# Eleven modulations of a two-layer diffusion block as scaled row sums on VectorE, ScalarE and GpSimd

## Chip, cores and metric

The kernel runs on one core of a Trainium2 chip. The metric is the device time of one execution in microseconds (us), as the median of three runs. Engines are named as the profile names them: PE is TensorE's matmuls, PEld its weight loads, DVE is VectorE, ACT is ScalarE, POOL is GpSimd, SP is SyncE, whose queue here only issues transfers. A name like L252 is line 252 of the kernel before; the changed kernel has other line numbers, and where its lines are named it is said.

## The reference, cut to what matters

Two layers run over 256 latent and 256 context tokens of width 1024. Every layer is a half-step gated feed-forward (FFN), a token mixer, and a second FFN. Shift, scale and gate of each come from nine modulations per layer, each a matrix-vector product with a 1024x1024 slice of `w_mod`, once for the latent tokens' vector `c` and once for the context tokens' vector `c_ctx`:

```
mx = (silu(c) @ w_mod[l] + b_mod[l]).reshape(BATCH, 9, 1, 1024)
mc = (silu(c_ctx) @ w_mod[l] + b_mod[l]).reshape(9, 1024)
hx = hx + 0.5 * mx[:, 2] * swiglu(modulate(hx, norm_g[l, 0], mx[:, 0], mx[:, 1]), ffn_w_gu[l, 0], ffn_w_down[l, 0])
...
def swiglu(x, w_gu, w_down):
    gate, up = jnp.split(x @ w_gu, 2, axis=-1)
    return (jax.nn.silu(gate) * up) @ w_down
```

In the second layer the context tokens are only read by the mixer, so its last modulations (index 5 and up) are needed for the latent tokens alone.

## The kernel before, in words

All 512 tokens lie in one tile, features on the partitions. A float32 matmul is done as three matmuls of type fp32r (`mm3`, L291 to L293): weights and activations are split into a rounded high part and the low remainder, and the three are high by high, high by low, and low by high. The first operand is the weight: L291 and L292 read the high half of the weight, `spl[:, 0]`, and only L293 its low half, `spl[:, 1]`.

The weights come through a single list of units, written by `plan`, in the order in which they are consumed:

- a `gu` unit is 128 gate columns and 128 up columns of `ffn_w_gu` (1 MB in two transfers); an FFN has 22 of them, and each feeds 48 matmuls into two accumulators, first the gate's 24, then the up's 24;
- a `down` unit is 256 columns of `ffn_w_down`; an FFN has three chunks of four, after gu 7, gu 15 and gu 21;
- a `mod` unit is 256 columns of one modulation (1 MB), four to a modulation; they are strewn as fillers between the `gu` and `down` units, in the FFNs' parts of the list one filler behind each.

`take` (consumption of a unit) does three things: it issues loads up to three units on from the one taken (`load_to`), makes sure that the unit's own weight is split (`split`, L251 the high part on ACT, L252 the low part on DVE, each in two halves of 128x1024), and calls `ahead`, which splits the next weight unit early. `ahead` looks at two units from the cursor on and no further:

```
j = self.cur
n = min(j + 2, len(self.units))
while j < n and not self.units[j][3]:
    j += 1
if j < n:
    self.split(j)
```

Units that need no split (`mod`) are stepped over. So with one filler between two weight units, taking weight unit i splits weight unit i+1.

In `ffn`, after the 48 matmuls of a gu, come the gate's silu on ACT (`sl`, L667, needs the gate's accumulator only), the product with the up accumulator on DVE (`hv`, L669, needs the last of the 48 matmuls), its rounded copy on ACT (`hid`, L671), its remainder on POOL (L672), and then `fillers`, which consumes all fillers up to the next weight unit. After a `down` unit come four residual updates on DVE (`resid`, L729, two for each of the two accumulators), then the fillers. Work of the S5 preparation and deferred pieces are put between the matmuls by `step`, five times per gu and about four times per down.

A mod unit (`mod_unit`, L467) is eight matmuls of 128x32 by 128x256 in four column strips, into one bank for the four units of a modulation; after the fourth, a copy to SBUF (`mev`, L471), two transposes (L486) and a few short DVE instructions (`mod_finish`) bring the sums into place.

Of the kernel before, what the change touches and what calls it, by code (L numbers as in the profile page):

```python
# [33 lines left out]
PI_LO = 3.1415925  # L34

# [58 lines left out]
class Net:  # L94
    def __init__(self, nc, tc, I, out, es):
# [19 lines left out]
        self.mh = c.tile([128, 8], F32, name="mh")  # L115
        self.mod = [c.tile([128, 9, KT, 2], F32, name=f"mod{l}") for l in range(2)]
# [4 lines left out]
        self.units = []  # L121
        self.bg = []
# [14 lines left out]
    def plan(self):  # L137
# [140 lines left out]

    def fillers(self):
        while self.cur < len(self.units) and self.units[self.cur][0] == "mod":  # L280
            self.mod_unit(*self.units[self.cur][1])

    def fill(self, n):
        while n and self.cur < len(self.units) and self.units[self.cur][0] == "mod":
            self.mod_unit(*self.units[self.cur][1])
            n -= 1
# [18 lines left out]
    def step(self, n=1):  # L305

        for _ in range(n):
            f = self.q.pop(0) if self.q else None
# [5 lines left out]
    def flush(self):  # L314
        while self.q:
            f = self.q.pop(0)
            if f is not None:
                f()

# [5 lines left out]
    def prologue(self):  # L325
        nc, I = self.nc, self.I
        self.norm_open()
        with lines(self.tc, name="pro", bufs=1) as pp:
# [12 lines left out]
            nc.vector.memset(self.mh, -0.5)  # L341
            self.small_rows(0, sm[0])
# [138 lines left out]

    def mod_finish(self, l, m, us, e):
# [10 lines left out]
        if m in (1, 4, 7):  # L493
            g0 = 72 + 8 * (m // 3)
            g = self.smT[l][:, g0 + k0:g0 + k1].unsqueeze(2)
            nc.vector.scalar_tensor_tensor(self.A[l][:, m // 3, k0:k1], dst, 1.0, bc(g, [128, 2 * n, 2]), op0=OP.add, op1=OP.mult)
        if m in (2, 8):
            nc.vector.tensor_scalar(dst, dst, 0.5, None, op0=OP.mult)
# [146 lines left out]
    def ffn(self, l, f, halves, started, nxt=None):  # L645
# [5 lines left out]
        with lines(self.tc, name=f"ffn{l}{f}", bufs=1) as fp:  # L651
            j0 = 0
            for ci, nf in enumerate(CH):
# [26 lines left out]
                early = None  # L680
                for u in range(4):
# [43 lines left out]
                j0 += nf  # L725

# [855 lines left out]
```

## Time and profile before

| what | value |
|---|---|
| median of three runs (lowest to highest) | 1961.87 us (1960.69 to 1962.42) |
| the profiled execution, its own time | 1962.65 us |
| its span, first to last instruction | 1960.7 us |
| mean granted TensorE clock, share of full | 0.988 |
| PE busy | 1907.6 us, 97% |
| DVE, ACT, POOL busy | 907.3, 678.8, 574.3 us |
| chain that ended last: PE, DVE, POOL | 84%, 6%, 4% |

The profiled execution lies 0.8 us above the median, and 1.95 us of its time lie outside the span. The layers follow one another: prologue to about 65 us, then FFN, mixer, FFN for each layer. Busy shares are averages over the span; the chain of work that ended last says which engine the end waits for.

### The profile page before, as it was taken

To read this page: it belongs to the slowest core of one execution; us is meant where nothing else is said; L and a number is where in the kernel's file an instruction comes from. 1 tells how busy PE (TensorE), PEld (TensorE's weight loads), DVE (VectorE), ACT (ScalarE), POOL (GpSimd) and SP (SyncE) were. 2 spreads that over 40 slices of the span, in tenths; PEclk is the share of its full clock that TensorE was granted. 3 is DMA by queue.
4 is the path that set the end of the run, shared out by engine and by line. 5 is a ranking of instruction groups with operands and counts; after the bars stand their busy time and mean duration, and the time that the engine had idled before them with its cause. 6 is when DMAs were issued, how large, how long until landed. Compare 5 with 4: busy or idle time off the path is not lost.

```text
span 1960.7 us, 28001 instructions
## 1 busy us (share of the span) xinstructions
PE 1907.6 (97%) x11345; PEld 1557.8 (79%) x11345; DVE 907.3 (46%) x1596; ACT 678.8 (35%) x1128; POOL 574.3 (29%) x661
## 2 busy tenths in 40 slices
PE   7999999999999999999999999999999988999999
PEld 4777777788896587788888877777788878579999
DVE  6453233246457835232333554423433745655555
ACT  4421222224355634222212342122223435445343
POOL 2137461124535032100101314746212545231000
PEclk9999999999999999999999999999999999799999
DMA  9656566534431024533232455656523453036563
GB/s 309 178 166 200 174 205 212 165 97 141 132 105 51 2 86 130 173 117 96 88 105 76 139 158 167 201 160 217 178 75 113 141 166 100 22 126 215 175 194 108
DMA packets 364100, 277.75 MB, mean 142 GB/s; under 512 B 29854, under 2 KB 355812, under 8 KB 363972
## 3 DMA queue, kind: packets, MB, share of 16 engines
q1 hardware_dynamic: 361008, 268.44, 44.3%
q0 software_dynamic: 1888, 7.31, 1.0%
q8 instruction: 89, 1.46, 0.3%
q10 hardware_dynamic: 1076, 0.22, 0.1%
q14 instruction: 39, 0.32, 0.0%
HBM read 263.39 MB, written 12.55 MB: 141 GB/s over the span
## 4 chain that ended last, share of the span: by engine, by line
PE 84%; DVE 6%; POOL 4%; DMA 2%; ACT 1%; SPq 1%; issue 1%; POOLq 0%; ACTq 0%; DVEq 0%
PE acc L291 24%; PE acc L292 24%; PE acc L293 23%; PE b L467 3%; PE acc L1458 2%; PE t L1490 1%; DVE xm L562 1%; PE t L1510 1%; POOL ss L1134 1%; DVE xn L572 1%; PE acc L1463 1%; POOL sqs L523 1%; PE t L1100 1%; DMA bias<-in_na_rpb 1%; DVE xn L570 1%
## 5 line engine op out<-in xcount | busy, mean ns | idle before, releaser
L291 PE MATMUL acc<-xn,spl 128*128 128x512 f32 (+1 forms) x1664 | 598.0, 359 | 8.2 <-ACT mv L1340 5.9
L292 PE MATMUL acc<-xn,spl 128*128 128x512 f32 (+1 forms) x1664 | 590.7, 355 | 1.9 <-DVE xn L396 0.2
L293 PE MATMUL acc<-xn,spl 128*128 128x512 f32 (+1 forms) x1664 | 587.3, 353 | 0.1
L252 DVE TENSOR_TENSOR spl<-raw,spl 128x1024 fp32r<-128x1024 f32 (+2 forms) x312 | 390.2, 1287 | 276.0 <-ACT spl L251 273.8
L251 ACT ACTIVATE spl<-raw 128x1024 fp32r<-128x1024 f32 (+3 forms) x344 | 324.0, 990 | 303.9 <-PE acc L293 159.6
L291 PEld LDWEIGHTS acc<-xn,spl 128*128 128x128 f32 x1664 | 315.1, 189 | 71.7 <-issue 17.8
L292 PEld LDWEIGHTS acc<-xn,spl 128*128 128x128 f32 x1664 | 315.3, 189 | 46.7 <-DVE xn L570 4.3
L672 POOL TENSOR_TENSOR hid<-hv,hid 128x512 fp32r<-128x512 f32 (+1 forms) x88 | 101.8, 1156 | 852.2 <-ACT hid L671 852.2
L293 PEld LDWEIGHTS acc<-xn,spl 128*128 128x128 f32 x1664 | 315.3, 189 | 44.7 <-DVE spl L252 0.9
L291 PE MATMUL acc<-hid,spl 128*128 128x512 f32 (+1 forms) x740 | 265.2, 358 | 0.0
L292 PE MATMUL acc<-hid,spl 128*128 128x512 f32 (+1 forms) x740 | 262.0, 354 | 0.0
L293 PE MATMUL acc<-hid,spl 128*128 128x512 f32 (+1 forms) x740 | 261.7, 354 | 0.0
L669 DVE TENSOR_TENSOR hv<-sl,acc 128x512 f32<-128x512 f32 (+1 forms) x88 | 54.7, 621 | 365.1 <-PE acc L293 353.4
L671 ACT ACTIVATE hid<-hv 128x512 fp32r<-128x512 f32 (+1 forms) x88 | 50.9, 579 | 382.0 <-DVE hv L669 382.0
L729 DVE SCALAR_TENSOR_TENSOR h<-acc,mod,h 128x256 f32<-128x256 f32 x192 | 85.0, 479 | 210.8 <-PE acc L293 210.8
L291 PEld LDWEIGHTS acc<-hid,spl 128*128 128x128 f32 x740 | 139.8, 189 | 25.2 <-issue 6.4
L293 PEld LDWEIGHTS acc<-hid,spl 128*128 128x128 f32 x740 | 139.9, 189 | 19.7
L292 PEld LDWEIGHTS acc<-hid,spl 128*128 128x128 f32 x740 | 140.0, 189 | 18.5
L252 POOL TENSOR_TENSOR spl<-raw,spl 128x768 fp32r<-128x768 f32 (+3 forms) x32 | 65.3, 2041 | 211.4 <-ACT spl L251 199.5
L291 PE MATMUL acc<-spl,xn 128*128 128x384 f32 (+1 forms) x322 | 111.5, 346 | 0.0
L292 PE MATMUL acc<-spl,xn 128*128 128x384 f32 (+1 forms) x322 | 106.9, 332 | 0.4 <-POOL spl L252 0.3
L293 PE MATMUL acc<-spl,xn 128*128 128x384 f32 (+1 forms) x322 | 106.5, 331 | 0.0
(358 smaller groups left out, 1996.8 us busy)
## 6 DMA issues: line engine op xcount, KB each, us to landing
raw<-in_ffn_w_gu SPq DMA_DIRECT2D x176, 512.0 KB
raw<-in_w_mod SPq DMA_DIRECT2D x64, 1024.0 KB
raw<-in_ffn_w_down SPq DMA_DIRECT2D x32, 1024.0 KB
raw<-in_ffn_w_down SPq DMA_DIRECT2D x16, 768.0 KB
raw<-in_w_in SPq DMA_DIRECT2D x16, 768.0 KB
pmod<-in_w_mod SPq DMA_DIRECT2D x8, 1024.0 KB
raw<-in_w_out SPq DMA_DIRECT2D x8, 1024.0 KB
cld<-CL POOLq DMA_DIRECT2D x8, 576.0 KB, 4.8
```

The source lines that it names most:

```text
L251: nc.scalar.activation(s[:, 0, a:b], raw[:, a:b], AF.Copy)
L252: (nc.gpsimd if mix and b == n else nc.vector).tensor_tensor(s[:, 1, a:b], raw[:, a:b], s[:, 0, a:b].bitcast(F32), op=OP.subtract)
L291: mm(out, sl[0], sr[0], start=start, stop=False)
L292: mm(out, sl[0], sr[1], start=False, stop=False)
L293: mm(out, sl[1], sr[0], start=False, stop=stop)
L467: nc.tensor.matmul(p[32 * j:32 * j + 32, 0:256], self.cs[:, k, 6 - 2 * w:38 - 2 * w], raw[:, k, :], start=(a == 0 and w == 0), stop=(a == ...
L523: nc.gpsimd.tensor_tensor(self.sq_sum[:, c], self.sq_sum[:, c], s[:, c], op=OP.add)
L669: nc.vector.tensor_tensor(hv[:, c], sl[:, c], pu[:, c], op=OP.mult)
L671: nc.scalar.activation(hd[:, 0, c], hv[:, c], AF.Copy)
L672: nc.gpsimd.tensor_tensor(hd[:, 1, c], hv[:, c], hd[:, 0, c].bitcast(F32), op=OP.subtract)
L729: self.nc.vector.scalar_tensor_tensor(self.h[:, n, c], ps[:, c], self.mod[l][:, gate, n, s:s + 1], self.h[:, n, c], op0=OP.mult, op1=OP.add)
L1458: mm(s, q[:, 256 + 128 * t:384 + 128 * t], k, start=True, stop=h >= 6)
```

## The change

Eleven of the eighteen modulations (`ELEM`) leave the PE path. Each of their fillers, one mod unit of 256 columns and all eight row blocks before, becomes two `dvm` units of 512 columns and two row blocks (0.5 MB each), in the same place of the list. They have buffers of their own, `draw` (three, in the pool of the FFN), in place of the three `raw` buffers shared with the weights.

A dvm unit multiplies each of its two row blocks by the vector's value of that partition: for the latent tokens with one DVE instruction that also adds to a running sum `dacc1`, for the context tokens with an ACT copy with a scale (in place in `draw`) and an addition on POOL into `dacc0`. After four units (one half of a modulation) `total` puts four matmuls of 128x32 by 128x256 on PE, which add up the 128 partitions against a column of ones, and ACT copies the result; `finish` transposes it twice and adds the bias. `total` runs eight steps after the unit, `finish` three later. The two modulations (1,5) and (1,7) do the latent tokens alone. In the S5 preparation some scratch tiles now share a buffer, to make room.

```diff
+ELEM = ((0, 2), (0, 4), (0, 3), (0, 5), (0, 7), (0, 6), (1, 0), (1, 4), (1, 3), (1, 5), (1, 7))
...
         def mod_units(l, m, us=range(4)):
             for u in us:
+                if (l, m) in ELEM:
+                    for v in (2 * u, 2 * u + 1):
+                        n0, k0 = m * 1024 + v // 4 * 512, v % 4 * 2
+                        src = I["w_mod"][l].rearrange("(k p) n -> p k n", p=128)[:, k0:k0 + 2, n0:n0 + 512]
+                        U.append(("dvm", (l, m, v), [(slice(0, 1024), 2, src)], False))
+                    continue
...
+            if kind == "dvm" and self.fp is None:
+                return
             if i < 10 and kind == "mod":
                 raw = self.prop.tile([128, 2048], F32, name="pmod", tag="pmod", bufs=5)
+            elif kind == "dvm":
+                raw = self.fp.tile([128, 1024], F32, name="draw", tag="draw", bufs=3)
...
     def step(self, n=1):
         for _ in range(n):
+            if self.dv:
+                g = self.dv.pop(0)
+                if g:
+                    g()
...
+    def dvm_unit(self, l, m, v):
+        nc = self.nc
+        half, r = v // 4, v % 4
+        raw = self.take("dvm", (l, m, v)).rearrange("p (k n) -> p k n", k=2)
+        ss = (1,) if l and m > 4 else (0, 1)
+        if r == 0:
+            self.dacc = {s: self.fp.tile([128, 512], F32, name=f"dacc{s}", tag=f"dacc{s}", bufs=2) for s in ss}
+        acc = self.dacc
+        for i in range(2):
+            c0, c1 = (self.cs[:, 2 * r + i, 6 + s:7 + s] for s in range(2))
+            first = r == i == 0
+            if first:
+                nc.vector.tensor_scalar(acc[1], raw[:, i], c1, None, op0=OP.mult)
+            else:
+                nc.vector.scalar_tensor_tensor(acc[1], raw[:, i], c1, acc[1], op0=OP.mult, op1=OP.add)
+            if 0 in ss:
+                x = acc[0] if first else raw[:, i]
+                nc.scalar.activation(x, raw[:, i], AF.Copy, scale=c0)
+                if not first:
+                    nc.gpsimd.tensor_tensor(acc[0], acc[0], x, op=OP.add)
...
+        def total():
+            p = self.tp()
+            for j in range(2):
+                for s in range(2):
+                    z = 0 if s in ss else 1
+                    nc.tensor.matmul(p[64 * j + 32 * s:64 * j + 32 * s + 32, 0:256], self.sel[:, z:z + 32], acc[1 if z else s][:, 256 * j:256 * j + 256], start=True, stop=True)
+            st["e"] = self.modp.tile([128, 256], F32, name="mev", tag="mev")
+            nc.scalar.activation(st["e"], p[:, 0:256], AF.Copy)
...
+        self.dv_flush()
+        self.dv += [None] * 7 + [total, None, None, finish]
```

`take` and `ahead` are as before, and the instructions come out in another order. In the names of the rows below, `acc` is an accumulator of PE, `spl` a split weight, `hv` and `sl` the FFN's product and silu, `raw` a weight as loaded, `draw` a modulation's rows as loaded, `h` the residual stream.

DVE before, first FFN of layer 0, gu 8 to gu 10 (the accumulators named are those of the up halves):

```order
L669 TENSOR_TENSOR hv_1716<-sl_1714,acc_1646 128x512
L252 TENSOR_TENSOR spl_1734<-raw_1731,spl_1734 128x1024 x2
L669 TENSOR_TENSOR hv_1805<-sl_1803,acc_1740 128x512
L252 TENSOR_TENSOR spl_1825<-raw_1822,spl_1825 128x1024 x2
L491 TENSOR_REDUCE mod0_86<-t_1841 128x16
L492 TENSOR_TENSOR mod0_86<-mod0_86,smT0_90 128x16
```

DVE in the changed kernel, the same place:

```order
L758 TENSOR_TENSOR hv_1806<-sl_1804,acc_1744 128x512
L266 TENSOR_TENSOR spl_1814<-raw_1811,spl_1814 128x1024 x2
L530 TENSOR_SCALAR dacc1_1820<-draw_1728,cs_84 128x512
L532 SCALAR_TENSOR_TENSOR dacc1_1820<-draw_1728,cs_84,dacc1_1820 128x512
L532 SCALAR_TENSOR_TENSOR dacc1_1820<-draw_1741,cs_84,dacc1_1820 128x512 x2
L758 TENSOR_TENSOR hv_1920<-sl_1918,acc_1837 128x512
L266 TENSOR_TENSOR spl_1928<-raw_1925,spl_1928 128x1024 x2
```

Both show a product `hv`, then a split. Which gu the split is for stands in the rows of PE.

PE before, where gu 9 (acc_1740) ends and gu 10 (acc_1830) begins:

```order
L293 MATMUL acc_1740<-xn_83,spl_1640 128x512
L467 MATMUL b_1540<-raw_1721,cs_84 32x256 x8
L291 MATMUL acc_1830<-xn_83,spl_1734 128x512
L292 MATMUL acc_1830<-xn_83,spl_1734 128x512
L293 MATMUL acc_1830<-xn_83,spl_1734 128x512
```

PE in the changed kernel, where gu 8 (acc_1744) ends and gu 9 (acc_1836) begins:

```order
L313 MATMUL acc_1744<-xn_83,spl_1717 128x512
L314 MATMUL acc_1744<-xn_83,spl_1717 128x512
L312 MATMUL acc_1836<-xn_83,spl_1814 128x512
L313 MATMUL acc_1836<-xn_83,spl_1814 128x512
L314 MATMUL acc_1836<-xn_83,spl_1814 128x512
```

Before, spl_1734 stands on DVE behind the product of gu 8 and is read by gu 10, a whole gu later. In the changed kernel spl_1814 stands behind the product of gu 8 and is read by gu 9, the very next matmul.

ACT in the changed kernel, behind the same gu 8:

```order
L756 ACTIVATE sl_1804<-acc_1743 128x512
L760 ACTIVATE hid_1808<-hv_1806 128x512
L265 ACTIVATE spl_1814<-raw_1811 128x1024 x2
L535 ACTIVATE dacc0_1819<-draw_1728,cs_84 128x512
L535 ACTIVATE draw_1728<-draw_1728,cs_84 128x512
L535 ACTIVATE draw_1741<-draw_1741,cs_84 128x512 x2
```

The high part of the next weight now stands behind the copy `hid`, which reads `hv`.

DVE behind the down units of that chunk, changed kernel (acc_1535 and acc_1536 are down unit 2, and spl_1617 is read by down unit 3, acc_1639 and acc_1640):

```order
L822 SCALAR_TENSOR_TENSOR h_82<-acc_1535,mod0_87,h_82 128x256 x2
L822 SCALAR_TENSOR_TENSOR h_82<-acc_1536,mod0_87,h_82 128x256 x2
L266 TENSOR_TENSOR spl_1617<-raw_1615,spl_1617 128x1024 x2
L530 TENSOR_SCALAR dacc1_1623<-draw_1520,cs_84 128x512
L532 SCALAR_TENSOR_TENSOR dacc1_1623<-draw_1520,cs_84,dacc1_1623 128x512
L532 SCALAR_TENSOR_TENSOR dacc1_1623<-draw_1533,cs_84,dacc1_1623 128x512 x2
L822 SCALAR_TENSOR_TENSOR h_82<-acc_1639,mod0_87,h_82 128x256 x2
```

Before, the split behind the residual updates of down unit 2 was that of gu 8, a whole unit further on; now it is that of down unit 3.

## Rows read from the trace of the kernel before

**Rows 1.** The page's first part: busy time, share and instructions of each engine.
```profile
PE 1907.6 (97%) x11345; PEld 1557.8 (79%) x11345; DVE 907.3 (46%) x1596; ACT 678.8 (35%) x1128; POOL 574.3 (29%) x661
```
**Rows 2.** Timeline 206 to 208 us: start, duration, engine, line, names, [idle before <- releaser].
```profile
206.17 0.39 PE L293 MATMUL acc<-xn,spl 128*128 128x512 f32 x1
206.49 1.07 PE L467 MATMUL b<-raw,cs 128*32 128x256 f32 x16
...
206.67 0.69 DVE L669 TENSOR_TENSOR hv<-sl,acc 128x512 f32<-128x512 f32 x1 [8.16 <-PE acc L293]
207.39 0.64 ACT L671 ACTIVATE hid<-hv 128x512 fp32r<-128x512 f32 x1 [2.46 <-DVE hv L669]
...
207.49 0.50 PE L291 MATMUL acc<-xn,spl 128*128 128x512 f32 x1
...
207.83 0.40 PE L292 MATMUL acc<-xn,spl 128*128 128x512 f32 x1
```
**Rows 3.** Timeline of PE, 209 to 210.5 us, around two transposes of a modulation.
```profile
209.47 0.39 PE L293 MATMUL acc<-xn,spl 128*128 128x512 f32 x1
209.70 0.38 PE L486 MATMUL t<-k,mev 128*128 128x128 f32 x2
209.84 0.48 PE L291 MATMUL acc<-xn,spl 128*128 128x512 f32 x1
```
**Rows 4.** Timeline of DVE, 195 to 221 us: the splits around that product.
```profile
195.90 2.62 DVE L252 TENSOR_TENSOR spl<-raw,spl 128x1024 fp32r<-128x1024 f32 x2 [1.65 <-ACT spl L251]
...
216.06 3.21 DVE L252 TENSOR_TENSOR spl<-raw,spl 128x1024 fp32r<-128x1024 f32 x2 [8.70 <-ACT spl L251]
```
**Rows 5.** Groups by line and shape: names, count, busy us, mean ns, idle before.
```profile
L252 DVE TENSOR_TENSOR spl<-raw,spl 128x1024 fp32r<-128x1024 f32 x252 | 327.3, 1338 | 220.5 <-ACT spl L251 218.7 <-issue 1.8
L729 DVE SCALAR_TENSOR_TENSOR h<-acc,mod,h 128x256 f32<-128x256 f32 x192 | 85.0, 479 | 210.8 <-PE acc L293 210.8
...
L251 ACT ACTIVATE spl<-raw 128x1024 fp32r<-128x1024 f32 x260 | 259.9, 1047 | 281.5 <-PE acc L293 146.8 <-DMA raw<-in_ffn_w_gu 58.8 <-issue 43.9
L671 ACT ACTIVATE hid<-hv 128x512 fp32r<-128x512 f32 x66 | 41.7, 632 | 319.6 <-DVE hv L669 319.6
...
L523 POOL TENSOR_TENSOR sqs<-sqs,sq 128x512 f32<-128x512 f32 x20 | 28.6, 1430 | 81.9 <-ACT sq L522 73.6 <-issue 8.0
```
**Rows 6.** Windows, gap and stretch behind: length, busy us (instructions) by engine, PEclk, DMA, GB/s.
```profile
537.30:540.00 2.70, 0.03 (x2) 0.01 (x2) 2.21 (x2) 0.00 (x0) 2.23 (x2) 0.92 0.00 0
540.00:547.00 7.00, 6.93 (x24) 6.44 (x25) 1.77 (x2) 3.04 (x5) 1.87 (x1) 0.54 0.60 175
598.60:602.00 3.40, 0.00 (x0) 0.00 (x0) 1.84 (x4) 1.18 (x4) 2.81 (x3) 0.85 0.00 0
602.00:609.00 7.00, 6.99 (x26) 5.68 (x27) 4.83 (x13) 4.19 (x7) 6.04 (x6) 0.58 0.00 0
...
1596.00:1598.30 2.30, 0.01 (x1) 0.00 (x0) 2.30 (x4) 0.00 (x0) 1.11 (x2) 1.00 0.21 77
1598.30:1605.00 6.70, 4.96 (x27) 4.16 (x28) 3.13 (x7) 1.99 (x3) 5.36 (x7) 0.75 0.01 1
...
1761.20:1762.80 1.60, 0.08 (x8) 0.06 (x8) 1.02 (x3) 1.00 (x2) 1.09 (x2) 1.00 1.11 361
1762.80:1769.00 6.20, 6.12 (x56) 5.34 (x57) 6.04 (x14) 3.81 (x8) 1.69 (x2) 1.00 1.12 336
```
**Rows 7.** Timeline of PE behind the gap that ended at 602 us.
```profile
603.02 0.63 PE L293 MATMUL acc<-xn,spl 128*128 128x512 f32 x1
603.45 0.63 PE L291 MATMUL acc<-xn,spl 128*128 128x512 f32 x1
```
**Rows 8.** Windows: the first FFN of layer 0 as a whole, columns as in rows 6.
```profile
70.00:480.00 410.00, 407.68 (x2329) 321.43 (x2322) 164.93 (x311) 116.35 (x166) 152.51 (x183) 1.00 0.54 170
```
**Rows 9.** Timeline of SP's queue, 199 to 222 us: the issue of a gu weight.
```profile
219.30 1.07 SPq L228 DMA_DIRECT2D raw<-in_ffn_w_gu  x2
```
**Rows 10.** Timeline of ACT, 205 to 232 us: the split that waited for that weight.
```profile
225.17 2.01 ACT L251 ACTIVATE spl<-raw 128x1024 fp32r<-128x1024 f32 x2 [4.27 <-DMA raw<-in_ffn_w_gu]
```

More of the change, by code (lines that the diff above doesn't have):

```diff
@@ L121, in __init__ @@
         self.units = []
+        self.dv = []
+        self.fp = None
         self.bg = []
@@ L277, in ahead, with filler @@
             self.split(j)
+    def filler(self):
+        if self.cur == len(self.units) or self.units[self.cur][0] not in ("mod", "dvm"):
+            return False
+        kind, key = self.units[self.cur][:2]
+        (self.mod_unit if kind == "mod" else self.dvm_unit)(*key)
+        return True
     def fillers(self):
-        while self.cur < len(self.units) and self.units[self.cur][0] == "mod":
-            self.mod_unit(*self.units[self.cur][1])
+        while self.filler():
+            pass
     def fill(self, n):
-        while n and self.cur < len(self.units) and self.units[self.cur][0] == "mod":
-            self.mod_unit(*self.units[self.cur][1])
+        while n and self.filler():
             n -= 1
@@ L318, in flush, with dv_flush @@
                 f()
+    def dv_flush(self):
+        while self.dv:
+            g = self.dv.pop(0)
+            if g:
+                g()
     def drain(self):
@@ L480, in mod_unit, with finish @@
             self.q.append(lambda: self.mod_finish(l, m, us, e))
+    def dvm_unit(self, l, m, v):
[18 more added lines that the diff above has]
+                    nc.gpsimd.tensor_tensor(acc[0], acc[0], x, op=OP.add)
+        if r < 3:
+            return
+        st = {}
+        def total():
[6 more added lines that the diff above has]
+            nc.scalar.activation(st["e"], p[:, 0:256], AF.Copy)
+        def finish():
+            q = self.tp()
+            for i in range(2):
+                nc.tensor.transpose(q[:, 128 * i:128 * i + 128], st["e"][:, i * 128:i * 128 + 128], self.ident)
+            k0 = 4 * half
+            dst = self.mod[l][:, m, k0:k0 + 4]
+            t = q[:, 0:256].rearrange("p (a j s r) -> p a j s r", a=2, j=2, s=2)[:, :, :, :, 0]
+            b = self.smT[l][:, m * 8 + k0:m * 8 + k0 + 4].rearrange("p (j a) -> p a j", a=2).unsqueeze(3)
+            nc.vector.tensor_tensor(dst.rearrange("p (j a) s -> p a j s", a=2), t, bc(b, [128, 2, 2, 2]), op=OP.add)
+            self.mod_derived(l, m, k0, k0 + 4)
+        self.dv_flush()
+        self.dv += [None] * 7 + [total, None, None, finish]
@@ L482, in mod_finish, with mod_derived @@
+    def mod_derived(self, l, m, k0, k1):
+        nc = self.nc
+        dst = self.mod[l][:, m, k0:k1, :]
+        if m in (1, 4, 7):
+            g0 = 72 + 8 * (m // 3)
+            g = self.smT[l][:, g0 + k0:g0 + k1].unsqueeze(2)
+            nc.vector.scalar_tensor_tensor(self.A[l][:, m // 3, k0:k1], dst, 1.0, bc(g, [128, k1 - k0, 2]), op0=OP.add, op1=OP.mult)
+        if m in (2, 8):
+            nc.vector.tensor_scalar(dst, dst, 0.5, None, op0=OP.mult)
     def mod_finish(self, l, m, us, e):
@@ L680, in ffn @@
                 early = None
+                if lastc:
+                    self.dv_flush()
                 for u in range(4):
```

18 lines of the change are left out of this document (10 added, 8 removed).

## Prediction

> **What bounds the kernel now.** The page comes first: PE is busy 97% of the span, no other engine half of it [rows 1]. Next I read the stretch that the change touches, the first FFN of layer 0: of 410 us PE is busy 407.7, and DVE 165, ACT 116 and POOL 153 are spare capacity [rows 8]. On that page alone the change looks sure to pay: it takes work from the full engine and gives it to idle ones. Then I read one seam between two gu units at the scale of single instructions [rows 2]. The last matmul of a gu starts at 206.17. DVE's product needs it and starts at 206.67, after 8.16 us of idling; ACT's copy follows at 207.39. PE meanwhile does a mod unit and starts the next gu at 207.49, because that gu's weight was split long before, from 195.90 to 198.52 [rows 4]. So PE is never held up by the chain product, copy, split. It would be if the split came behind the product. That is what decides here.
>
> **What is removed.** A mod unit holds up PE as follows: from the last L293 at 206.17 to the next L291 at 207.49 are 1.32 us, and to the L292 behind it another 0.34 [rows 2]. Undisturbed, one matmul follows the other by 0.23 us (209.47 to 209.70) [rows 3]. So it costs 1.32 - 0.23 + 0.34 - 0.23 = 1.2 us. Eleven modulations have 44 of them: -53 us. Each was on PE's path, for PE is dense there [rows 8].
>
> **What is added on PE.** Each half modulation, 22 in all, adds up partitions with four matmuls of 128x32 by 128x256; a mod unit has eight of them in 1.07 us [rows 2], so 0.54 us, and with the 0.11 us by which the next matmul comes late, 0.65. 22 of them: +14 us. The pair of transposes costs 209.84 - 209.47 - 0.23 = 0.14 and some 0.1 behind it [rows 3]; there are 22 pairs and were 11: +2.6 us. PE alone gains 53 - 14 - 2.6 = **36 us**.
>
> **What is added elsewhere.** DVE gets 16 multiply-adds of 128x512 per modulation, 176. Nothing like them stands in the trace; the nearest are the product on 128x512 at 0.69 us [rows 2] and the residual update on 128x256 at 0.479, doubled 0.96 [rows 5]. I take 0.8: 141 us on an engine that is 46% busy. ACT gets 144 scaled copies at 0.632 [rows 5], 91 us; POOL 126 additions at 1.43 [rows 5], 180 us. In the first FFN, with six of the modulations, that is 77, 61 and 120 us beside 165, 116 and 153 in more than 410 us [rows 8]: each engine has room. Their cover is PE's work; none of it is on the path by volume. The order matters more.
>
> **The split comes late.** `ahead` looks at two units. With one filler behind a gu it reaches the next gu; with two dvm units it does not. So the next weight is split only when the first dvm unit is taken, which stands behind the gu's product on DVE and behind its copy on ACT. The orders above show it for gu and for down units.
>
> Behind a gu, with PE's last matmul starting at 206.17: product until 207.36, copy until 208.03 [rows 2], high half on ACT 1.05 us, until 209.1 [rows 5], low half on DVE 1.34 us, until 210.4 [rows 5]. L291 and L292 can start at 209.1; L293, which needs the low half, at 210.45. Undisturbed, that L293 would have started three steps of 0.23 behind 206.17, at 206.86. PE loses **3.5 us** (3.2 if splits and copies touch). The second half of the split is ready 1.3 us later, while PE has nine more matmuls, 2.1 us, before it needs it. Nothing else is queued on PE there.
>
> Behind a down unit ACT is free and does the high half in time. On DVE the last two residual updates start 0.5 us behind 206.17 and take 0.96, the low half 1.34 [rows 5]: 209.0 against 206.86, so **2.15 us**.
>
> From the plan's list: of the 44 pairs, 32 stand behind a gu (16 in the first FFN of layer 0, 4 in its second, 12 in the first of layer 1) and 12 behind a down unit. 32 x 3.5 + 12 x 2.15 = **138 us**. Both engines take their instructions in order: in the rows nothing passes the waiting product. The Trainium skill says so as a rule (TensorE: Matmul & The Clock Gate, "Architectural detail"): ScalarE and VectorE are strict FIFOs. By it the 138 us stand; if the split could pass the product, only the -36 would be left.
>
> **PE's clock.** Each of those waits leaves PE idle from 206.6 to 209.1, 2.5 us, then busy with two matmuls, then idle for 0.7 more. Such gaps exist in the trace [rows 6]. Behind 2.7, 3.4 and 2.3 us the granted clock of the next 7 us was 0.54, 0.58 and 0.75, and matmuls followed each other by 0.43 us in place of 0.23 [rows 7]: the lower of the two levels, 1.2 instead of 2.4 GHz. Behind a gap of 1.6 us it stayed at 1.00. The gap at 598.60 is the nearest: dense matmuls on both sides. Of the 7 us behind it 42% are lost, 2.9 us. My wait is between the two kinds, as two matmuls lie in it; its 3.2 us of idling are nearer the upper. I let the clock fall in two of three of the 32: 21 x 2.9 = **62 us**, and in none of the 12. The ends are 0 and 44 x 2.9 = 128. [...]
>
> **Transfers.** Bytes are the same. The weights have three buffers for themselves, but SP's queue is in order, and a weight stands behind a `draw` that waits until POOL has released the one three before. That release comes about 9.5 us behind the gu's end (split 5.6, two multiply-adds, two scaled copies partly beside them, two additions of 1.43); a weight landed 4.8 us after its issue had ended [rows 9, 10]. Together 15 to 16 us, against the 16.5 us until the next split wants it (11.1 us of matmuls, 3.5 of waiting, 1.9 to the split). Barely covered: 0 in the sum, up to 1 us in each of 32, +32, at the upper end, if POOL is late.
>
> **Sum.** The profiled execution took 1962.65 us, 0.04% above the median. 1962.65 - 36 + 138 + 62 = **2127 us**, +8.4%.
>
> **Rivals.**
> - *The waits without the clock.* Two matmuls inside each wait may be enough to hold it: 1962.65 - 36 + 138 = 2065. For it: the 1.6 us gap at full clock. Against: 2.3 us was enough at 1596. Chance 0.25.
> - *POOL and the transfers decide.* If draws come free late, weights do too and each wait grows: 2127 + 32, and with the clock lost behind nearly every wait up to 2205. For it: POOL's release chain above. Against: POOL has over 100 us spare in the first FFN [rows 8]. Chance 0.15.
> - *The waits do not appear, and PE's saving shows.* Place: the split's position behind the product. If DVE and ACT finish the split before PE has ended the gu, only -36 is left: 1927 us. It decides from an average of 36 / 44 = 0.8 us per pair; below that the kernel gets faster. For it: PE at 97% and idle engines. Against: the product needs the up half's last matmul, and DVE's idle time before it ends with just that, 8.16 us on PE's L293 [rows 2]. Chance 0.06.
> - *Nothing changes*, because waits and saving cancel within 0.2%, some 4 us (what a measurement of this kernel can tell from no change): 0.01.
>
> **Numbers.** The forecast has what is left, 0.53. Slower by over 0.2%: 0.53 + 0.25 + 0.15 = 0.93; same 0.01; faster 0.06. The range takes in the waits at their shorter value without the clock (32 x 3.2 + 12 x 2.15 = 128, so 2055) and the third case up to 2205. Outside lie the faster case and a little on either side.
>
> **What would show it.** In the changed profile PE should wait in its 32 places for ACT's and DVE's split of `spl` (about 2.5 and 0.7 us), and in 12 for DVE's alone; before it hardly ever waits for them. DVE's long idle before `hv` on PE stays, the one before the split goes. The strip of PE's clock, 9s before, should fall to 7 or 8 in the slices of the first FFNs of both layers (3 to 9 and 24 to 29) and stay in the others. Wrong would be the count of pairs, if PE waits elsewhere; the 3.5 us, if the wait per pair differs; the 62 us, if the clock stays at 1.00 there. If the end comes below 1960, the order read above did not bind.

## The result and the profile after

The changed kernel takes 2189.14 us in the median (2185.16 to 2195.32), the kernel before on the same chip 1961.61 us (1960.69 to 1962.42): a ratio of 1.1163, interval 1.1136 to 1.119. It is slower, by 228 us; 2127 had been forecast, in a range of 2055 to 2205. The profiled execution took 2195.32 us. The profile page of the changed kernel, parts 1 and 2, engines and clock:

```profile
span 2193.5 us, 27710 instructions
...
PE 1984.7 (90%) x10839; PEld 1600.1 (73%) x10839; DVE 1109.0 (51%) x1777; ACT 784.7 (36%) x1283; POOL 767.9 (35%) x789
...
PEclk9888888899999999989999998888899999899999
```

PE was busy for 1907.6 us [rows 1] and is for 1984.7, though 11 modulations less pass through it; that is the first sign of the clock. Its idle time went from 53 to 209 us (span less busy time). A slice of the strip is 55 us here. The 8s stand in slices 2 to 8, most of the first FFN of layer 0, in 18, its second, and in 25 to 29, the first of layer 1. The strip of before is 9 in all of these; both have one 7 or 8 in slice 35. Slice 18, with 4 of the 44 pairs, was not among those that the forecast named. The windows view of the first FFN's stretch, columns as in [rows 6]:

```profile
70.00:480.00 410.00, 325.52 (x1319) 242.87 (x1319) 206.82 (x321) 143.89 (x198) 236.29 (x234) 0.87 0.44 136
```

Against [rows 8], PE's busy time there is 325 in place of 408 us. 1319 matmuls in place of 2329 were done; some of the missing ones are the modulations' own, but of the three of `mm3` alone it is 1105 in place of 1659. What PE waits for stands in its list of waits of the changed kernel (engine, tile, line, what it waits for; us in total, times, longest):

```profile
PE acc L312 <- ACT spl L265: 116.7, 40, 5.5
PE acc L314 <- DVE spl L266: 31.2, 41, 1.6
PE t L1064 <- POOL CL L1057: 8.8, 2, 5.0
```

The two splits hold 148 us of the 156 us of new idle time. In the list of the kernel before, waits for a split come to about 1 us; the longest line is this:

```profile
PE t L292 <- DVE spl L252: 0.8, 1, 0.8
```

One seam between two gu units, in the timeline of the changed kernel, set against [rows 2]:

```profile
122.75 0.40 PE L314 MATMUL acc<-xn,spl 128*128 128x512 f32 x1
...
122.98 0.38 PE L554 MATMUL b<-k,mev 128*128 128x128 f32 x2
123.28 0.69 DVE L758 TENSOR_TENSOR hv<-sl,acc 128x512 f32<-128x512 f32 x1 [2.94 <-PE acc L314]
124.00 0.63 ACT L760 ACTIVATE hid<-hv 128x512 fp32r<-128x512 f32 x1 [4.92 <-DVE hv L758]
124.54 1.99 ACT L265 ACTIVATE spl<-raw 128x1024 fp32r<-128x1024 f32 x2
...
125.61 2.58 DVE L266 TENSOR_TENSOR spl<-raw,spl 128x1024 fp32r<-128x1024 f32 x2 [1.64 <-ACT spl L265]
...
125.63 0.50 PE L312 MATMUL acc<-xn,spl 128*128 128x512 f32 x1 [2.27 <-ACT spl L265]
...
127.12 0.80 PE L314 MATMUL acc<-xn,spl 128*128 128x512 f32 x1 [0.75 <-DVE spl L266]
127.71 0.63 PE L312 MATMUL acc<-xn,spl 128*128 128x512 f32 x1
128.14 0.63 PE L313 MATMUL acc<-xn,spl 128*128 128x512 f32 x1
```

Product, copy, high half, low half: the chain is read off line by line. From the last L314 of the old gu to the first L314 of the new one are 127.12 - 122.75 = 4.37 us. Less the 0.69 of three undisturbed steps and the 0.24 of the two transposes, 3.4 us are lost; the forecast had 3.5. Behind it matmuls follow each other by 0.43 us: half clock.

### The profile page after: what moved, and what is told of

It is laid out like the page before. It is cut to its first block, busy times and chain, and to the rows that moved or that the text cites. A ratio compares the mean times of both kernels' runs of the same rounds, so it can differ in the third digit from the quotient of the medians.

```text
span 2193.5 us, 27710 instructions
## 1 busy us (share of the span) xinstructions
PE 1984.7 (90%) x10839; PEld 1600.1 (73%) x10839; DVE 1109.0 (51%) x1777; ACT 784.7 (36%) x1283; POOL 767.9 (35%) x789
## 5 line engine op out<-in xcount | busy, mean ns | idle before, releaser
L312 PE MATMUL acc<-xn,spl 128*128 128x512 f32 (+1 forms) x1664 | 625.3, 376 | 96.3 <-ACT spl L265 87.9
L314 PE MATMUL acc<-xn,spl 128*128 128x512 f32 (+1 forms) x1664 | 617.2, 371 | 20.7 <-DVE spl L266 20.7
L313 PE MATMUL acc<-xn,spl 128*128 128x512 f32 (+1 forms) x1664 | 611.6, 368 | 1.9 <-DVE xn L429 0.2
L312 PEld LDWEIGHTS acc<-xn,spl 128*128 128x128 f32 x1664 | 329.0, 198 | 164.9 <-ACT spl L265 98.7
L314 PEld LDWEIGHTS acc<-xn,spl 128*128 128x128 f32 x1664 | 327.4, 197 | 89.0 <-DVE spl L266 40.0
L313 PEld LDWEIGHTS acc<-xn,spl 128*128 128x128 f32 x1664 | 329.1, 198 | 54.6 <-DVE xn L658 4.3
L312 PE MATMUL acc<-hid,spl 128*128 128x512 f32 (+1 forms) x740 | 273.3, 369 | 28.8 <-ACT spl L265 28.8
L314 PE MATMUL acc<-hid,spl 128*128 128x512 f32 (+1 forms) x740 | 270.0, 365 | 10.5 <-DVE spl L266 10.5
L313 PE MATMUL acc<-hid,spl 128*128 128x512 f32 (+1 forms) x740 | 268.8, 363 | 0.0
L537 POOL TENSOR_TENSOR dacc<-dacc,draw 128x512 f32<-128x512 f32 x126 | 187.2, 1485 | 158.7 <-ACT draw L535 106.8
L312 PEld LDWEIGHTS acc<-hid,spl 128*128 128x128 f32 x740 | 144.0, 195 | 55.4 <-ACT spl L265 32.5
L314 PEld LDWEIGHTS acc<-hid,spl 128*128 128x128 f32 x740 | 144.3, 195 | 37.4 <-DVE spl L266 16.5
L532 DVE SCALAR_TENSOR_TENSOR dacc<-draw,cs,dacc 128x512 f32<-128x512 f32 x154 | 164.0, 1065 | 4.7
L313 PEld LDWEIGHTS acc<-hid,spl 128*128 128x128 f32 x740 | 144.5, 195 | 20.0
L535 ACT ACTIVATE draw<-draw,cs 128x512 f32<-128x512 f32 x126 | 91.0, 724 | 131.4 <-DVE dacc L532 83.2
```

Source lines behind the costliest of these rows:

```text
L312: mm(out, sl[0], sr[0], start=start, stop=False)
L313: mm(out, sl[0], sr[1], start=False, stop=False)
L314: mm(out, sl[1], sr[0], start=False, stop=stop)
L532: nc.vector.scalar_tensor_tensor(acc[1], raw[:, i], c1, acc[1], op0=OP.mult, op1=OP.add)
L535: nc.scalar.activation(x, raw[:, i], AF.Copy, scale=c0)
L537: nc.gpsimd.tensor_tensor(acc[0], acc[0], x, op=OP.add)
```

## The experiments

The theory was: the late split costs its waits and the clock behind them, and the added work lies beside PE. The rivals: the added work itself (GpSimd, transfers) is what costs; or the waits cost without the clock. Below, "idle" is the span less PE's busy time, and "half clock" is the time that PE is busy in stretches that the trace lists at the lower level; half of that is what the clock costs. Each ratio is to runs of the kernel before that were taken with that kernel.

| kernel | median us | ratio to before | PE idle, us | busy at half clock, us |
|---|---|---|---|---|
| before | 1961.61 | 1 | 53 | 44 |
| changed | 2189.14 | 1.1163 [1.1136, 1.119] | 209 | 238 |
| e1_early | 2037.53 | 1.0385 [1.0368, 1.0402] | 134 | 89 |
| e2_before_late | 2094.09 | 1.0679 [1.0659, 1.0699] | 135 | 119 |
| e3_warm | 2179.49 | 1.1101 [1.1081, 1.1121] | 144 | 116 |
| e4_no_ctx | 2149.93 | 1.0952 [1.0932, 1.0973] | 188 | 186 |
| e5_early_no_ctx | 1952.0 | 0.9945 [0.9932, 0.9958] | 69 | 66 |
| e7_ctx_on_dve | 2002.2 | 1.0203 [1.0186, 1.022] | 110 | 75 |
| e11_early_later | 2010.38 | 1.025 [1.0236, 1.0265] | 109 | 84 |
| e12_weight_first | 2002.31 | 1.0216 [1.0196, 1.0236] | 105 | 75 |
| e6_layer1 | 1960.23 | 0.9988 [0.9979, 0.9998] | 61 | 57 |
| e8_layer1_scratch | 1960.13 | 0.9997 [0.9988, 1.0006] | 58 | 55 |
| e10_layer1_later | 1949.53 | 0.9942 [0.9928, 0.9956] | 52 | 55 |
| e9_scratch | 1962.18 | 1.0004 [0.9996, 1.0013] | 54 | 45 |

### The late split undone, and the late split alone

**e1_early** keeps all added work and lets the split and the loads look past the dvm units:

```diff
-            self.load_to(i + 3)
+            self.load_to(self.past(i + 3, i + 1))
...
-        n = min(j + 2, len(self.units))
+        n = min(self.past(j + 2, j), len(self.units))
...
+    def past(self, n, j):
+        while j < len(self.units) and self.units[j][0] == "dvm":
+            j += 1
+        return max(n, j + 1)
```

Of the units that one call loads, those that need a split now go first.

> The changed kernel with one thing undone: taking a gu or down unit looks past the dvm units, loads the next weight (ahead of the draws that are due with it) and splits it at once, so that the split stands ahead of the product on VectorE again. All of the added work on VectorE, ScalarE and GpSimd stays. Theory (the late split and the clock behind its waits are the loss): the waits for spl go, the granted clock is back at 0.98 or more, and PE's saving of 36 us shows: 1920 to 1945 us. Rival (the added work itself, by volume, by GpSimd's slowness in freeing draws, or by contention, is the loss): 2080 us or more, with the waits for spl still there. A transfer that lands late now and then would show between them, at 1950 to 2020.

2037.53 us lies between the two. The late split, with its clock, is 2189 - 2037.5 = 152 us of the loss; weights that landed late are in this too, since e1 also loads them ahead of the draws. Some 76 us remain, and with them the 35 us or so that PE saves, which is used up as well. PE's waits in e1:

```profile
PE t L1069 <- POOL CL L1062: 40.3, 7, 10.4
...
PE acc L317 <- ACT spl L265: 11.1, 5, 4.1
PE t L1092 <- POOL BL L1083: 9.3, 4, 4.3
```

The waits for splits of weights in FFNs fell from 148 to some 20 us (VectorE's are shorter lines of the list); those for `CL` rose from 8.8 to 40.3. `CL` and `BL` are tiles that GpSimd makes in the S5 preparation, work that runs in the first FFN of each layer, among the fillers; the longest two waits for `CL` lie at 205 us and, in layer 1, at 1325 us. GpSimd's timeline in e1 shows three additions between one `CL` and the next:

```profile
203.77 1.40 POOL L1062 TENSOR_TENSOR CL<-te,te 128x576 f32<-128x576 f32 x1
205.13 3.94 POOL L542 TENSOR_TENSOR dacc<-dacc,draw 128x512 f32<-128x512 f32 x3
...
211.38 1.40 POOL L1062 TENSOR_TENSOR CL<-te,te 128x576 f32<-128x576 f32 x1
```

The windows from 80 to 250 us, before and in e1, show how full GpSimd is there:

```profile
80.00:250.00 170.00, 170.00 (x937) 130.07 (x936) 68.18 (x170) 42.94 (x57) 80.30 (x123) 1.00 0.57 182
```

```profile
80.00:250.00 170.00, 131.33 (x574) 101.98 (x573) 113.05 (x204) 62.74 (x88) 128.55 (x145) 0.89 0.50 144
```

The fifth busy time is POOL's: 80 of 170 us before, 129 in e1, while PE drops from 170 to 131. A second limit had stood behind the first.

**e2_before_late** is the kernel before with nothing but the late split, at the same 44 fillers:

```diff
         j = self.cur
+        if j < len(self.units) and self.units[j][0] == "mod" and self.units[j][1][:2] in ELEM:
+            return
```

> The kernel before with the late split alone: behind the same 44 fillers the next weight is split only when the filler is taken, so behind the product; the modulations stay on TensorE and nothing is added to VectorE, ScalarE or GpSimd. Each wait is shortened by the mod unit that PE does in it, about 1.1 us. Theory: 32 x (3.5 - 1.2) + 12 x (2.15 - 1.2) = 85 us more, and little of the clock lost, since PE is idle for some 1.3 us and not 2.5 at a stretch: 2030 to 2060 us, clock 0.97 or more. Rival (the added work is the loss): 1962 us, as before.

2094.09 us, 133 more than before and above both. Its waits of PE:

```profile
PE acc L294 <- ACT spl L252: 47.7, 32, 1.8
PE acc L296 <- DVE spl L253: 33.8, 46, 2.4
```

81.5 us, as the expectation had it (here a mod unit of about 1 us fills part of each wait, so 1.5 us are left in place of 2.3). What it had not counted is the clock. A seam of e2 in PE's timeline:

```profile
122.38 0.50 PE L294 MATMUL acc<-xn,spl 128*128 128x512 f32 x1 [1.49 <-ACT spl L252]
...
123.86 0.59 PE L296 MATMUL acc<-xn,spl 128*128 128x512 f32 x1 [0.75 <-DVE spl L253]
124.25 0.63 PE L294 MATMUL acc<-xn,spl 128*128 128x512 f32 x1
124.68 0.63 PE L295 MATMUL acc<-xn,spl 128*128 128x512 f32 x1
```

After 1.49 and 0.75 us of idling the matmuls follow each other by 0.43 us. The trace lists 30 stretches at half clock, 7 before, and 119 us of busy time in them in place of 44: 38 us lost to the clock. Waits and clock make 119 of the 133 us. Most of the rest is longer records: PE's busy time, taken at full clock, is 1956.2 - 59.6 = 1896.6 us in e2 and 1907.6 - 21.9 = 1885.7 before, for the same matmuls. So the late split alone, without any of the added work, makes the kernel slower by a ratio of 1.068.

### The clock

**e3_warm** puts ten matmuls of no use ahead of each weight unit that comes behind dvm units:

```diff
+    def warm(self, p):
+        if self.units[self.cur - 2][0] == "dvm":
+            for _ in range(10):
+                self.nc.tensor.matmul(p, self.xn[:, 0, 0, 0:128], self.xn[:, 0, 0, :], start=True, stop=True)
```

> The changed kernel with ten needless matmuls of 128x128 by 128x512 (2.3 us) ahead of each of the 44 weight units that follow a pair of dvm units, into the accumulator that the unit then overwrites. They fill the wait for the split and change nothing of it. Theory (the clock is lost through the idle time): the granted clock comes back to about 0.985, and the time falls by the 97 us that the lower clock costs by the two traces: 2080 to 2110 us, although TensorE does more. Rival (the clock is lost for another reason, or the waits are bound by something that grows with TensorE's speed): no change or slower by up to 44 x 2.3 = 101 us, 2189 to 2290.

2179.49 us, far above the expectation. The reason stands in the trace: time at half clock went from 238 to 116 us, so 61 us came back, and idle time went down by 65. But 440 matmuls by 0.23 us are 101 us, in place of 65 us of idling; the rest pushed the next units back. 61 + 65 - 101 = 25 us; the span of the profiled execution fell by 22. So the clock's cost is of the size that the trace's stretches give, and ten matmuls at each place cost most of what they give back: 10 us are left in the median.

### The context half: ScalarE's copies and GpSimd's additions

**e4_no_ctx** leaves out the context tokens' half of every dvm unit, **e5_early_no_ctx** does so in e1. The edit is the same in both:

```diff
-        ss = (1,) if l and m > 4 else (0, 1)
+        ss = (1,)
```

> The changed kernel without the context tokens' half of the eleven modulations (their products are left out, so those modulations are the bias alone): no scaled copies on ScalarE, no additions on GpSimd; draws are freed by VectorE. The late split stays. Theory (order, not volume): the 44 waits stay at 3.2 and about 2 us; only what late transfers add to them goes, 20 to 30 us of idling and perhaps as much of clock: 2140 to 2175 us. Rival (GpSimd's chain and the transfers behind it carry the loss): 2100 us or less.

> The early split of e1_early and, besides, the context tokens' half of the eleven modulations left out (those modulations are the bias alone): no scaled copies on ScalarE, no additions on GpSimd. Of e1_early's 76 us above the kernel before, its trace puts the waits on GpSimd: TensorE waits 40 us for CL and 9 us for BL of the S5 preparation, which stand behind the additions in GpSimd's queue, and 12 us for the copies mev. Theory (late split first, GpSimd's queue second): both are gone, TensorE's saving of 36 us is left, 1920 to 1945 us, clock 0.985 or more. Rival (VectorE's multiply-adds or the lesser TensorE work does not save what was worked out): 1955 us or more.

e4: 2149.93 us, as the theory had it. With the late split in place, the whole of ScalarE's and GpSimd's added work is worth 39 us. PE's waits in e4 say where:

```profile
PE acc L312 <- ACT spl L265: 91.8, 37, 4.0
```

The waits for ACT's split are 25 us less than 116.7. It is the long ones that went: in the changed kernel 12 of 40 are over 3 us, in e4 4 of 37. At eight of the twelve a weight landed late (see e11 and the section on why). e5: 1952.0 us, between its two expectations. It is faster than the kernel before (it leaves half of the moved work out), but 16.5 us of waits for `CL` are left in its list of waits. PE's busy time, taken at full clock, is 1884 - 33 = 1851 us in e5 and 1908 - 22 = 1886 before: the change saves 35 us on PE, where 36 were forecast. In e5 the rest of it goes into 16 us of idling and 11 of clock.

**e7_ctx_on_dve** is e1 with the context half computed on VectorE, as the latent half is, so that ACT and POOL have none of it:

```diff
-                x = acc[0] if first else raw[:, i]
-                nc.scalar.activation(x, raw[:, i], AF.Copy, scale=c0)
-                if not first:
-                    nc.gpsimd.tensor_tensor(acc[0], acc[0], x, op=OP.add)
...
+                nc.vector.scalar_tensor_tensor(acc[0], raw[:, i], c0, acc[0], op0=OP.mult, op1=OP.add)
```

> The early split with the context tokens' sums on VectorE too, as multiply-adds like those of the latent tokens, so that ScalarE's copies and GpSimd's additions are gone and the result is whole. VectorE gets about 320 multiply-adds in all. Theory (GpSimd's queue was the second bound): GpSimd's waits go; 1925 to 1960 us if VectorE keeps up. Rival (VectorE becomes the bound in the stretch of the S5 preparation: 68 us busy of 170 before, 8 multiply-adds of about 0.8 us for each of some 13 pairs more): products and splits come late again, 1970 to 2040 us.

2002.2 us: the rival. PE's waits:

```profile
PE t L1068 <- POOL CL L1061: 29.6, 4, 12.2
PE acc L319 <- DVE spl L266: 21.4, 10, 3.7
```

Now VectorE is late with the low half, and `CL` stays late though GpSimd got nothing new. The windows of e7 from 80 to 250 us show VectorE busy for 148 of 170 us:

```profile
80.00:250.00 170.00, 141.65 (x666) 110.40 (x665) 147.64 (x263) 38.64 (x52) 94.05 (x119) 0.94 0.55 159
```

One way by which that reaches `CL` stands in the time that GpSimd takes for the same 120 instructions on `te`, a tile of the preparation, from 60 to 480 us (busy us and count, clock, DMA), before and in e7:

```profile
60.00:480.00 420.00, 91.07 (x120) 1.00 0.55 172
```

```profile
60.00:480.00 420.00, 107.56 (x120) 0.96 0.57 165
```

They take 16 us longer beside the busier VectorE, and in e5, which also has no additions on GpSimd, 107.0 us (the last section shows the same of single instructions). GpSimd also waits 31 us for VectorE's `Pn` over the run; the kernel before had 24 of that and no wait for `CL`. In that stretch neither engine has room for all of the added work.

### The preparation and the transfers

**e11_early_later** is e1 with PE coming to `CL` ten filler steps later, and to the other places four later:

```diff
+                    for _ in range(10 if d == hg == 0 else 4):
+                        yield
```

> The kernel with the early split and all eleven modulations, in which TensorE comes to CL ten filler steps later and to BL four steps later. Theory: its 40 us of waits for CL and 9 us for BL were TensorE coming too early to a GpSimd that gets there in the end; without them and part of the clock behind them 1950 to 1990 us. Rival: GpSimd's queue is full over the stretch, so that the same lateness turns up as waits for other tiles: 2010 us or more.

2010.38 us, just inside the rival's range. The waits for `CL` and `BL`, 50 us in e1, are gone from the list; 27 us of time came back. Others took their place:

```profile
PE acc L317 <- ACT spl L265: 23.4, 9, 6.3
```

SP's queue and ACT around one of them, both e11:

```profile
207.91 3.12 SPq L243 DMA_DIRECT2D draw<-in_w_mod  x2
211.07 1.09 SPq L243 DMA_DIRECT2D raw<-in_ffn_w_gu  x2
...
218.11 2.00 ACT L265 ACTIVATE spl<-raw 128x1024 fp32r<-128x1024 f32 x2 [2.09 <-DMA raw<-in_ffn_w_gu]
```

Two draws take 3.12 us to issue (two weight transfers 1.09), because one waits for its buffer; the weight goes out behind them and lands after ACT wanted it. In the changed kernel SP's queue stands for 545.6 us in 61 places behind POOL's addition:

```profile
SPq L242 <- POOL dacc L537: 545.6, 61, 28.5
```

**e12_weight_first** is e11 and issues each of these weights one unit earlier still, ahead of such draws:

```diff
-            self.load_to(self.past(i + 3, i + 1))
+            n = self.past(i + 3, i + 1)
+            if any(u[0] == "dvm" for u in self.units[i + 1:n]) and self.fp is not None:
+                n = self.past(n, n)
+            self.load_to(n)
```

> The kernel with the early split and TensorE's later steps to CL and BL, in which each gu or down weight is issued one unit earlier still, ahead of the draws that wait for GpSimd. Theory: what was left of the loss, 23 us of waits for ScalarE's split and 16 us for VectorE's, are weights that landed late because they stood behind such draws in SP's queue; without them and the clock behind them 1965 to 1985 us. Rival: the transfers themselves or the engines are full there, so that draws or other tiles are late instead: 2000 us or more.

2002.31 us: the rival. Now the draws are late. The queue, DVE and PE at the same place in e12:

```profile
209.20 9.06 SPq L243 DMA_DIRECT2D draw<-in_w_mod  x2
...
210.65 3.12 DVE L540 SCALAR_TENSOR_TENSOR dacc<-draw,cs,dacc 128x512 f32<-128x512 f32 x2 [9.94 <-DMA draw<-in_w_mod]
...
215.50 3.44 DVE L266 TENSOR_TENSOR spl<-raw,spl 128x1024 fp32r<-128x1024 f32 x2
...
215.52 0.79 PE L320 MATMUL acc<-xn,spl 128*128 128x512 f32 x1 [8.48 <-ACT spl L265]
```

DVE waits 9.94 us for a draw. The next split of a weight stands in line behind that wait, on DVE and, behind the scaled copies, on ACT; PE waits 8.48 us for it. Lateness only moves, from `CL` to weights to draws: in none of e1, e11 and e12, where GpSimd releases the draws, do the first FFNs take their share of the eleven modulations at PE's pace. Whether more buffers or a faster GpSimd would change that was not tried.

### The same method where there is room

**e9_scratch** is the kernel before with the shared scratch tiles alone, to see whether these cost anything:

```diff
-            t4 = [pp.tile([128, 16, 16], F32, name=f"bt{i}") for i in range(4)]
+            t4 = [pp.tile([128, 4, 144], F32, name=f"bt{i}", tag=f"tmp{i}").rearrange("p a b -> p (a b)") for i in range(2)]
```

> The kernel before with the shared S5 scratch tiles of the change alone; the modulations and the split stay as before. Theory (shared scratch holds up GpSimd's chain): two waits for CL of some 3 us and the clock behind them, 1968 to 1976 us. Rival (CL is late in e6_layer1 for another reason): 1962 us, no CL wait.

1962.18 us: no difference, and no wait for `CL` in its list. The shared scratch costs nothing by itself.

**e6_layer1** splits early and moves only the five modulations of layer 1, as fillers of the second FFN of layer 0, where no S5 preparation runs; layer 0's stay on PE. **e8_layer1_scratch** is e6 with the scratch tiles of before. The cut shows two of the places changed against the changed kernel.

```diff
-ELEM = ((0, 2), (0, 4), (0, 3), (0, 5), (0, 7), (0, 6), (1, 0), (1, 4), (1, 3), (1, 5), (1, 7))
+ELEM = ((1, 0), (1, 4), (1, 3), (1, 5), (1, 7))
...
-                mods = [(1, m, [u]) for m in (1, 0) for u in range(4)]
+                mods = [(1, m, [u]) for m in (1, 0, 4, 3, 5, 7) for u in range(4)]
```

> The early split, with only the five modulations of layer 1 off TensorE, all of them as fillers of the second feed-forward of layer 0, where no S5 preparation runs and GpSimd is nearly idle; the six of layer 0 are mod units on TensorE as in the kernel before. Five elevenths of 36 us can be saved: 16 us. Theory: nothing else is late, 1942 to 1952 us. Rival (the additions or the transfers hold the weights up in any stretch): 1962 us or more.

> e6_layer1 with the S5 preparation's scratch tiles of the kernel before (four of their own, which fit since the draws now lie in a feed-forward without that preparation). In e6_layer1 TensorE waited twice for CL, 6.6 us, in the feed-forwards that hold no dvm unit, and the clock fell behind. Theory (the shared scratch holds up GpSimd's chain there): the CL waits go and with them about 10 us: 1944 to 1952 us. Rival (CL is late for another reason, or the five modulations save less than worked out): 1956 us or more.

1960.23 and 1960.13 us, both within 0.2% of before and slower than expected. A wait for `CL` stays, with either scratch; e8:

```profile
PE t L1067 <- POOL CL L1060: 6.8, 2, 3.4
```

It lies in layer 1's first FFN, whose fillers have left. PE gets to `CL` sooner there, and GpSimd's chain, which has no added work in it, is not done.

**e10_layer1_later** is e8 and lets PE come to `CL` eight steps later:

```diff
+                    for _ in range(8 if d == hg == 0 else 0):
+                        yield
```

> The kernel of layer 1 alone with the scratch of before, in which TensorE takes the first multiplications of the block that lead to CL eight filler steps later, so that GpSimd's chain has had time to write CL. If CL is late because TensorE comes to it too early, the two waits of 3.4 us go, with the clock that falls behind them: 1946 to 1953 us. Rival: GpSimd's chain is late by more than eight steps, or the time is held elsewhere: 1957 us or more, with the waits for CL still there or in another place.

1949.53 us, ratio 0.9942 [0.9928, 0.9956], as the theory had it: 0.4 us are left of the waits for `CL`. This kernel computes all that the one before does and is faster than it and than the changed one. Five modulations on the idle engines are worth 11 us, of the 16 that five elevenths of PE's 35 us would be. PE's busy time, taken at full clock, is 1898.2 - 27.7 = 1870.5 us, 15 below before; the clock takes some 6 of these back.

## Why the prediction was right, and where it was off

The direction, the mechanism and the place were right; 2189 lies in the range, 62 us above the forecast, and nearer to the range's upper end, which belongs to the second rival. The loss of the profiled execution's span, 2193.5 - 1960.7 = 233 us, is 156 of idle PE, plus 97 by which the clock's cost grew (119 - 22), less 20. Step by step:

- **What is removed and added on PE: right.** -36 us forecast, 35 measured in e5. In the changed kernel only 20 show. Matmuls beside a wait have longer records (0.50 us in the seam above, in place of 0.39), two for each of 44 seams at least; in e2, with the matmuls of before, such records make PE's busy time 11 us longer at as many seams.
- **The added work's durations: too low on the average.** The rows of the changed kernel by form:

```profile
L537 POOL TENSOR_TENSOR dacc<-dacc,draw 128x512 f32<-128x512 f32 x126 | 187.2, 1485 | 158.7 <-ACT draw L535 106.8 <-issue 44.8
...
L532 DVE SCALAR_TENSOR_TENSOR dacc<-draw,cs,dacc 128x512 f32<-128x512 f32 x154 | 164.0, 1065 | 4.7
```

  The multiply-add takes 1.065 us in the mean, above even the upper bound of 0.96; the copy 0.72 (0.632 forecast), the addition 1.49 (1.43). The 0.8 that was taken is close for a multiply-add that runs while GpSimd does nothing, 0.75; the forecast left out that VectorE and GpSimd lengthen each other's instructions (last section). What this cost in the changed kernel was not tried apart.
- **The late split, 138 us: right in its size.** 3.4 us in the seam shown, forecast 3.5; 81 waits in all, 148 us. Less the 23 us of the next point these are 125 us of idling, and with the longer records of the first point (11 us in e2, the 16 missing here) 136 to 141. The same mechanism alone (e2) moved the time by 133 us, and taken away (e1) by 152, the clock included.
- **Transfers, 0 in the sum: wrong, by some 15 us.** "Barely covered" was not covered. Of PE's 40 waits for ACT's split in the changed kernel, 12 are over 3 us, and what they have above the 2.4 of a plain seam adds up to 23 us. At eight of them, 15 us, ACT itself had idled until the weight landed; one reads, in ACT's and PE's timeline of the changed kernel:

```profile
210.26 2.01 ACT L265 ACTIVATE spl<-raw 128x1024 fp32r<-128x1024 f32 x2 [10.61 <-DMA raw<-in_ffn_w_down]
...
211.37 0.50 PE L312 MATMUL acc<-hid,spl 128*128 128x512 f32 x1 [4.74 <-ACT spl L265]
```

  This seam lies behind a down unit. There the forecast had ACT in time; of the 12 such places PE waited for ACT at eight, 25 us in all, each time for a weight that had landed late. In e4, which leaves POOL's additions out, four waits over 3 us and 5 us of excess are left. The forecast had named this path, POOL's release and the weight behind the draw in SP's queue, and had priced it at its lower end. The argument from POOL's spare volume was the weak one: a release that comes late is a matter of order, not of volume. At the other four of the twelve, 8 us, the weight was there, but VectorE came late to the product, behind instructions of the S5 preparation. One of these seams, PE and DVE:

```profile
103.47 0.40 PE L314 MATMUL acc<-xn,spl 128*128 128x512 f32 x1
...
106.56 0.69 DVE L758 TENSOR_TENSOR hv<-sl,acc 128x512 f32<-128x512 f32 x1
```

  The product starts 3.1 us after the last matmul has started, 0.5 us in the seam shown first. With the split behind the product, PE waits for that too.
- **The clock, 62 us: right in kind, too low.** It cost 97 us more than before. The two assumptions that kept it low both fell: that two matmuls inside the wait hold the clock a third of the time, and that the 12 places behind a down unit lose nothing. Stretches at half clock lie at 41 of the 44 seams, at all 32 behind a gu and at nine of the 12 behind a down unit; each costs 97 / 41 = 2.4 us, where 2.9 were taken. The Trainium skill (TensorE: Matmul & The Clock Gate, "HAM oscillation") describes a loop that waits some 3 to 5 us for data in every tile and starts every tile at the low clock. Here the clock fell behind every gu after shorter waits, 2.2 us and more for ACT's half; with the still shorter ones of e2 it fell at about half of the seams: 23 more stretches than before for 44.
- **The first rival, waits without the clock (2065)**, is out by the strip of the clock and by e3. **The second, POOL and transfers**, was part of the truth, not in place of the late split but on top of it: its times, 2159 to 2205, hold the 2189, and the forecast's 2127 does not come near. With the 23 us of longer waits and the clock at its measured cost the sum would have been 2127 + 23 + 35 = 2185.
- **The third rival, that PE's saving shows**, is what e5, with half of the moved work, and e10, with five modulations, are: it does, once the split is early and GpSimd's order leaves room.

What the prediction did not see is the limit behind the first one: in the first FFN of each layer the S5 preparation on GpSimd comes behind the additions and takes longer beside VectorE's multiply-adds (e5, e7), and PE then waits for `CL`. The forecast's "each engine has room" was an addition of busy times, as if the engines did not touch each other. Without the late split the kernel would still have been slower (e1, 1.0385).

## What to carry to other kernels

Before moving work from a full engine to idle ones, look at the instruction next to the seam, not at the shares: what a look-ahead reaches by count of units changes when a unit is cut in two, and a split that stood a unit ahead comes to stand behind the result it used to overlap. Spare volume on an in-order engine is no spare time; ask what each added instruction stands in front of, which queue waits for the buffer that it frees, and whether a neighbour's instructions grow longer beside it. Where the idle engine does have room, move only so much (here five of eleven modulations) and move the consumer of its other results back as far as the added work makes them late.

## What the runs showed of the hardware

The clock fell behind shorter idling than the trace before had led to think. There it had stayed at 1.00 behind a gap of 1.6 us [rows 6]; in e2 it fell, at about half of the seams, behind 1.49 us, two matmuls, and 0.75 us more. The windows of the changed kernel behind the seam at 125.6 us give its size, 0.62 and 0.70, then full:

```profile
125.60:129.00 3.40, 2.62 (x7) 1.79 (x8) 3.35 (x4) 0.98 (x2) 0.38 (x1) 0.62 0.00 0
129.00:136.00 7.00, 7.00 (x23) 5.55 (x22) 4.18 (x5) 3.43 (x5) 6.02 (x5) 0.70 0.22 63
136.00:139.00 3.00, 3.00 (x15) 2.46 (x14) 0.84 (x2) 0.00 (x0) 0.92 (x2) 1.00 1.10 310
```

VectorE and GpSimd lengthen each other's instructions. Of the changed kernel's 154 multiply-adds of 128x512 with a value for each partition, 69 ran while GpSimd did nothing, and all of these took 0.74 to 0.75 us; the 13 that ran wholly beside GpSimd instructions took 1.93 us in the mean. One place, four multiply-adds in a row (the first line is the same row in a window that ends at 129 us) and the GpSimd additions that begin in the middle of it:

```profile
128.12 1.52 DVE L532 SCALAR_TENSOR_TENSOR dacc<-draw,cs,dacc 128x512 f32<-128x512 f32 x2
```

```profile
128.12 4.00 DVE L532 SCALAR_TENSOR_TENSOR dacc<-draw,cs,dacc 128x512 f32<-128x512 f32 x4
```

```profile
129.74 6.28 POOL L537 TENSOR_TENSOR dacc<-dacc,draw 128x512 f32<-128x512 f32 x4 [3.76 <-ACT draw L535]
```

The first two take 0.76 us each, the other two 2.48 us together. GpSimd's addition took 1.29 us in the mean where VectorE did nothing (44 of 126) and 1.65 wholly beside it (36); VectorE's low half of a split, 1.22 (161 of 252) and 1.73 (20). The product `hv` (0.69 us) and the residual update (0.48), which read an accumulator of PE, took the same beside GpSimd as without it. In e11 only 23 of the 154 multiply-adds ran while GpSimd did nothing, and their mean is 1.27 us. So a mean from a trace is not the price of an instruction on an idle chip: undisturbed, the multiply-add's 0.75 stands beside 0.69 for a product [rows 2] and 0.48 for the multiplication by such a value alone (14 of 22 in the changed kernel).
